# The latents' feed-forward by one level of Strassen's algorithm, in a two-layer diffusion backbone on one core

## The chip, the cores and the metric

The kernel runs on one core of one Trainium2 chip. A core has TensorE (matrix products, from SBUF into PSUM), VectorE, ScalarE and GpSimd (elementwise work; GpSimd reaches SBUF alone) and SyncE, whose queue issues all of this kernel's transfers. In the profile they are PE, DVE, ACT, POOL and SP; PEld is TensorE's loading of weights. The metric is the device time of one execution in microseconds (us). Before the change the median of three runs is 3615.9 us (3615.09 to 3621.17).

## The reference

Two layers work on 1024 latent tokens ("latents") of width 1024 and 256 context tokens. Each layer is an attention mixer and a convolutional feed-forward, each followed by a residual and a LayerNorm, with shift, scale and gate vectors that a small projection of the conditioning vector gives ("modulation"). The change is in the feed-forward, of inner width 2816:

```python
def conv_ffn(h, w_gate, w_up, conv_w, conv_b, w_down):
    g = h @ w_gate
    gp = jnp.pad(g, ((0, 0), (1, 1), (0, 0)))
    g = gp[:, :-2] * conv_w[0] + gp[:, 1:-1] * conv_w[1] + gp[:, 2:] * conv_w[2] + conv_b
    return (jax.nn.silu(g) * (h @ w_up)) @ w_down
```

Around it stand `h_l = xl * (1.0 + sc2_l) + sh2_l` and `xl = layer_norm(ALPHA * xl + gt2_l * f_l, ln2_g[i], ln2_b[i])`. Layer 0 does this for latents and context with the same weights, layer 1 for the latents alone, as only they are returned. All is float32.

## The kernel before

Activations lie with features on the 128 partitions and tokens along the free axis, in three tiles (`TT`): tile 0 and tile 1 are 512 latents each, tile 2 the 256 context tokens. A product in float32 is made of three faster ones: each operand is split into a rounded high part (`hi`, a ScalarE copy, L82) and the rest (`lo`, a subtraction on GpSimd or another engine, L85), and `gemm3` (L90) adds high times high, high times low and low times high in PSUM, every matmul at L88. So each weight block costs a split of 128x1024 (`weight`, L198), and each normalized tile is kept as two tiles (`b0h`, `b0l` for tile 0, `b1*`, `b2*` for the others).

A layer runs so:

- `mixer_pass` (L1046) makes the output projection of the mixer into the residual `acc`; in layer 0 for tiles 2 and 0, and then for tile 1.
- `mixer_norm` (L1078) queues the LayerNorm of each tile (`norm`, L316; `norm_parts`, L395) on a list `behind`. Each `gemm3` step calls `tick` (L100), which emits one step of the first norm in that list: the norms run behind matmuls. In layer 0 tile 2's norm is queued ahead of tile 0's.
- `conv_ffn` (L1097) loops over 22 blocks of 128 inner features. For each block it makes gate and convolution inputs per tile (`gate`, L1130), the convolution on VectorE (`conv`, L1141), up and the product with it, split again (`hidden`, L1148), and then the way down, whose 8 results per tile are added to `acc` by VectorE (`down`, L1157, L1170). Inner values never leave SBUF. The latents take 2*2*8*3 = 96 matmuls of 512 columns for gate and up in each block and 2*8*3 = 48 for the way down; the context takes 72 of 256 columns.
- In layer 0 the modulation vectors of layer 1 are summed on VectorE within that loop (`mod_vectors`, L161; L176), from 96 pieces of `w_mod`.
- At the end of layer 0 `finish` (L1188) queues the norms for the next mixer; `odd_begin` starts it with tiles 0, 2, 1. At the end of layer 1 the last tile is cut in two halves, so that the norm that nothing covers has 256 columns (`final`, L1173).

A planner orders each engine's instructions from this program by priority and by when it expects their inputs; `ahead` raises the priority of weights' loads. It also places the semaphore waits. The order on an engine is fixed when the kernel is built.

Of the kernel before, what the change touches and what calls it, by code (L numbers as in the profile page):

```python
# [12 lines left out]
F32 = mybir.dt.float32  # L13
# [5 lines left out]
P = 128  # L19
# [31 lines left out]
class Net:  # L51
# [109 lines left out]
    def mod_vectors(self, l, chunks, wpool, ppool, ptag):  # L161
# [3 lines left out]
        for which, half, cs in chunks:  # L165
            acc = {c: self.t(wpool, [P, 512], tag=f"mv{c}", bufs=1) for c in cs}
            c0 = 1024 * which + 512 * half
            for k in range(KT):
                w = self.t(wpool, [P, 512], tag="wm", bufs=2)
# [96 lines left out]
    def spread(self, tmp, ppool, ptag, r, nb, room=4, pbufs=None):  # L266

        nc = self.nc
        dg = self.t(tmp, [P, room, P], tag="diag", bufs=1)
# [125 lines left out]
    def norm_parts(self, t, eps, v, keep, done=None):  # L395
# [21 lines left out]
        if done is not None:  # L417
            done()

# [658 lines left out]
def mixer_norm(N, l, t):  # L1078

    scale = ALPHA if l == 0 else 1.0  # L1080
    N.behind.append((t, N.norm_parts(t, LN_EPS / scale**2, N.aff[t // 2], True)))
# [7 lines left out]
def mixer_out(N):  # L1089
    mixer_begin(N, 0)  # L1090
    for tiles in ((2, 0), (1,)):
        drain(mixer_pass(N, 0, tiles, N.qq, "f"))
        for t in tiles:
            mixer_norm(N, 0, t)


def conv_ffn(N, l):  # L1097
    nc, ins = N.nc, N.ins
    qq = N.qq
    sf = N.pool("scratch_f")  # L1100
    tiles = (0, 2, 1) if l == 0 else (0, 1)
    last = NF - 1
    tail = last if l == 0 else last - 1
    sm = N.pool("scratch_m")
    width = 1026 if l else 1284
    base = [1, 513, 1027]
    edges = [0, 1025] + ([] if l else [1026, 1283])
    cw = lambda i, f: N.vecs[:, V_CW + 66 * l + 22 * i + f : V_CW + 66 * l + 22 * i + f + 1]
    cb = lambda f: N.vecs[:, V_CB + 22 * l + f : V_CB + 22 * l + f + 1]
    hidh = N.t(sf, [P, TOK], F32R, tag="hidh", bufs=1)  # L1110
    hidl = N.t(sf, [P, TOK], F32R, tag="hidl", bufs=1)
    s = N.t(sf, [P, width], tag="s", bufs=1)
    for c in edges:
        nc.vector.memset(s[:, c : c + 1], 0.0)

    def padded():
        g = N.t(sf, [P, width], tag="g", bufs=2)
        for c in edges:
            nc.vector.memset(g[:, c : c + 1], 0.0)
        return g  # L1120

    def gemm(wt, t, c0=0, w=None):
        w = w or TT[t][1]
        ps = N.t(qq, [P, 512], tag="f")
        hh, hl = N.h[t]
        N.gemm3(ps[:, :w], [(wt[0][:, k * P : (k + 1) * P], wt[1][:, k * P : (k + 1) * P],
                             hh[:, k, c0 : c0 + w], hl[:, k, c0 : c0 + w]) for k in range(KT)])
        return ps[:, :w]

    def gate(wt, t, f, g, begin=True, s=s):  # L1130
        c = slice(base[t], base[t] + TT[t][1])
        ps = gemm(wt, t)
        nc.scalar.activation(g[:, c], ps, AF.Copy)
        if begin:
            nc.scalar.activation(s[:, c], ps, AF.Identity, scale=cw(1, f), bias=cb(f))

    def begin(t, f, g):
        c = slice(base[t], base[t] + TT[t][1])
        nc.scalar.activation(s[:, c], g[:, c], AF.Identity, scale=cw(1, f), bias=cb(f))

    def conv(f, g, s=s):  # L1141
        n = width - 2
        for sh, i in ((0, 0), (2, 2)):
            nc.vector.scalar_tensor_tensor(s[:, 1 : 1 + n], g[:, sh : sh + n], cw(i, f), s[:, 1 : 1 + n],
                                           op0=ALU.mult, op1=ALU.add)
        nc.scalar.activation(s[:, 1 : 1 + n], s[:, 1 : 1 + n], AF.Silu)

    def hidden(ps, t, c0=0, eng=None, out=None, s=s):  # L1148
        w = ps.shape[-1]
        t0 = TT[t][0] + c0  # L1150
        y = s[:, base[t] + c0 : base[t] + c0 + w]
# [21 lines left out]
    def final(wd, t, c0, w):  # L1173
# [3 lines left out]
        for m, _ in enumerate(down(wd, t, c0, w)):  # L1177
            if m % 2:
                next(steps)
# [675 lines left out]
```

## Time and profile before

| what | us |
| --- | --- |
| median of 3 runs | 3615.9 |
| the profiled execution | 3614.6 |
| its span, first to last instruction | 3612.8 |
| last matmul of layer 0's output projection | 903.4 |
| first feed-forward, last matmul | 1886.7 |
| last matmul of layer 1's output projection | 2809 |
| second feed-forward, last matmul of the way down | 3582.4 |
| mean clock granted to TensorE | 0.971 |

A row of a group gives line, engine, operation, what it writes <- what it reads, shapes and the count; behind the bar the busy time and the mean duration of one in ns; behind the next the idle time before them and who ended it. A row of the timeline begins with the start and the duration in us. In the view by stretches each engine has its busy time in the stretch and, in brackets, its instructions. Matmuls overlap each other, so the time that one costs is the distance from start to start.

### The profile page before, as it was taken

Reading aid. Unit: us, or ns where it says so; the run is one execution under the profiler, and the core shown is the slowest. Engines: PE = TensorE matmul, PEld = TensorE weight load, DVE = VectorE, ACT = ScalarE, POOL = GpSimd, SP = SyncE. Lnnn points to the kernel's source line nnn. Section 1 sums busy time; section 2 is a strip of 40 time slices with the busy share of each in tenths; the row PEclk is TensorE's granted clock in tenths of the full one; section 3 lists DMA queues with packets and bytes.
Section 4 is the critical chain, followed back from the end, with each engine's and each line's share of the span. In section 5 each row is a group of like instructions: output and inputs, shape, how many; then the busy total and the mean of one; then the engine's idle time right before and its main releaser. Section 6 shows DMA issues by size and latency. Waiting matters only on the chain.

```text
span 3612.8 us, 47500 instructions
## 1 busy us (share of the span) xinstructions
PE 3377.0 (93%) x17736; PEld 2779.2 (77%) x17736; DVE 2201.4 (61%) x3938; ACT 1428.1 (40%) x2667; POOL 1283.0 (36%) x956
## 2 busy tenths in 40 slices
PE   8998999999799999999987999998998999999996
PEld 4566778887688888888866888877886688888885
DVE  2137878865567556565455477777996544444445
ACT  3126778853422222222223355556774322222222
POOL 4244433324622222222247133445334522222224
PEclk9999999999999999999988999999999999999997
DMA  7666142332112222121113845557543111111111
GB/s 224 198 212 185 65 101 68 81 115 70 36 59 88 70 77 79 62 76 38 39 43 103 255 139 155 152 164 216 165 131 126 53 41 53 47 47 47 47 47 47
DMA packets 203864, 363.03 MB, mean 100 GB/s; under 512 B 16432, under 2 KB 102896, under 8 KB 202096
## 3 DMA queue, kind: packets, MB, share of 16 engines
q1 hardware_dynamic: 203632, 359.98, 32.6%
q8 instruction: 140, 2.29, 0.3%
q14 instruction: 92, 0.75, 0.1%
HBM read 284.61 MB, written 75.30 MB: 100 GB/s over the span
## 4 chain that ended last, share of the span: by engine, by line
PE 56%; POOL 7%; DVE 5%; issue 3%; ACT 3%; DMA 2%; SPq 0%; POOLq 0%; ACTq 0%; DVEq 0%
PE f L88 45%; PE tp L88 4%; PE s L88 2%; PE o L88 2%; POOL affy L405 1%; POOL acc L346 1%; PE tp L467 1%; POOL wl L85 1%; DVE stat L1573 1%; DVE p L1587 1%; DVE ptl L85 1%; POOL acc L413 1%; POOL sum L336 1%; ACT wh L82 1%; POOL acc L216 1%
## 5 line engine op out<-in xcount | busy, mean ns | idle before, releaser
L1170 DVE SCALAR_TENSOR_TENSOR acc<-f,modv,acc 128x512 f32<-128x512 f32 (+1 forms) x856 | 551.1, 691 | 398.2 <-PE f L88 396.2
L85 POOL TENSOR_TENSOR wl<-wraw,wh 128x1024 fp32r<-128x1024 f32 x122 | 299.4, 2454 | 925.7 <-ACT wh L82 925.6
L82 ACT ACTIVATE wh<-wraw 128x1024 fp32r<-128x1024 f32 x167 | 175.9, 1054 | 605.0 <-PE f L88 554.3
L88 PE MATMUL f<-b1h,wh 128*128 128x512 f32 (+1 forms) x848 | 338.4, 399 | 7.7 <-ACT wh L82 4.1
L88 PE MATMUL f<-b1l,wh 128*128 128x512 f32 (+1 forms) x848 | 337.0, 397 | 8.7 <-DVE b1l L85 8.6
L88 PE MATMUL f<-b1h,wl 128*128 128x512 f32 (+1 forms) x848 | 336.6, 397 | 2.7 <-DVE wl L85 2.7
L88 PE MATMUL f<-b0h,wh 128*128 128x512 f32 x784 | 313.4, 400 | 9.7 <-ACT wh L82 9.7
L88 PE MATMUL f<-hidl,wdh 128*128 128x512 f32 (+1 forms) x848 | 316.4, 373 | 3.0 <-POOL hidl L85 3.0
L88 PE MATMUL s<-k,q 128*128 128x512 f32 (+2 forms) x1152 | 305.7, 387 | 14.4 <-ACT sxc L1563 6.6
L88 PE MATMUL f<-hidh,wdh 128*128 128x512 f32 (+1 forms) x848 | 318.1, 375 | 0.2 <-ACT hidh L82 0.2
L88 PE MATMUL f<-b0h,wl 128*128 128x512 f32 x784 | 312.1, 398 | 5.0 <-POOL wl L85 5.0
L88 PE MATMUL f<-hidh,wdl 128*128 128x512 f32 (+1 forms) x848 | 315.1, 372 | 0.0
L88 PE MATMUL f<-b0l,wh 128*128 128x512 f32 x784 | 312.4, 398 | 0.0
L85 DVE TENSOR_TENSOR ptl<-tp,pth 128x512 fp32r<-128x512 f32 x412 | 279.6, 684 | 41.2 <-ACT pth L471 35.5
L471 ACT ACTIVATE pth<-tp 128x512 fp32r<-128x512 f32 x412 | 241.9, 594 | 104.0 <-PE tp L467 96.7
L467 PE MATMUL tp<-ident,p 128*128 128x128 f32 x1648 | 257.3, 276 | 20.3 <-DVE ptl L85 10.1
L467 PEld LDWEIGHTS tp<-ident,p 128*128 128x128 f32 x1648 | 197.4, 142 | 52.3 <-DVE ptl L85 10.3
L1153 DVE TENSOR_TENSOR s<-s,f 128x512 f32<-128x512 f32 (+1 forms) x112 | 69.8, 626 | 275.4 <-PE f L88 269.3
L88 PE MATMUL o<-pth,v 128*128 128x256 f32 x976 | 232.4, 300 | 4.6 <-ACT pth L471 4.4
L85 POOL TENSOR_TENSOR hidl<-s,hidh 128x512 fp32r<-128x512 f32 (+1 forms) x103 | 121.8, 1184 | 300.4 <-ACT hidh L82 287.7
L88 PEld LDWEIGHTS s<-k,q 128*128 128x128 f32 (+1 forms) x1152 | 188.7, 192 | 43.6 <-ACT p L1576 9.9
L88 PEld LDWEIGHTS f<-b1l,wh 128*128 128x128 f32 x848 | 162.3, 191 | 49.9 <-DVE b1l L85 14.4
(392 smaller groups left out, 8124.6 us busy)
## 6 DMA issues: line engine op xcount, KB each, us to landing
wm<-w_mod SPq DMA_DIRECT2D x192, 256.0 KB, 3.4
wraw<-w_gate SPq DMA_DIRECT2D x44, 512.0 KB, 3.5
wraw<-w_up SPq DMA_DIRECT2D x44, 512.0 KB, 3.5
wraw<-w_down SPq DMA_DIRECT2D x44, 512.0 KB, 3.5
k<-k SPq DMA_DIRECT2D x32, 640.0 KB, 5.3
v<-v SPq DMA_DIRECT2D x16, 1280.0 KB, 8.5
wraw<-w_in SPq DMA_DIRECT2D x39, 512.0 KB, 4.4
wraw<-w_out SPq DMA_DIRECT2D x32, 512.0 KB, 3.6
```

The lines of the kernel that those rows point to most:

```text
L82: return self.nc.scalar.activation(out, src, AF.Copy)
L85: (eng or self.nc.gpsimd).tensor_tensor(out, src, hi.bitcast(F32), op=ALU.subtract)
L88: self.nc.tensor.matmul(out, lhsT, rhs, start=start, stop=stop)
L216: nc.gpsimd.tensor_tensor(r[:rows, :w], r[:rows, :w], sin, op=ALU.mult)
L336: eng.tensor_tensor(new, acc[g], src, op=ALU.add)
L346: nc.gpsimd.tensor_tensor(x[k], x[k], c[:, :w], op=op)
L405: nc.gpsimd.tensor_scalar(y[:, :w], x, v[:, 0, k : k + 1], v[:, 1, k : k + 1], op0=ALU.mult, op1=ALU.add)
L413: nc.gpsimd.tensor_scalar(x, x, v[:, 2, k : k + 1], v[:, 3, k : k + 1], op0=ALU.mult, op1=ALU.add)
L467: nc.tensor.transpose(ps[:, n * P : (n + 1) * P], pt[:, kc : kc + P], N.ident[:, :])
L471: nc.scalar.activation(h[:, : n * P], ps[:, : n * P], AF.Copy)
L1153: nc.vector.tensor_tensor(y, y, ps, op=ALU.mult)
L1170: nc.vector.scalar_tensor_tensor(a, ps[:, :w], gt[:, m : m + 1], a, op0=ALU.mult, op1=ALU.add)
```

## The change

The feed-forward of the latents is written as two products of 2x2 blocks. On the way up the left matrix has gate and up weights as its rows and the two halves of the input features as its columns; the right matrix has the two halves of the features as rows and tiles 0 and 1 as columns. On the way down the halves are those of the inner width and of the output features. Each such product takes seven products of halves (Winograd's form, P1 to P7), of sums of blocks, in place of eight.

- `norm_operands` builds, in tile 1's norm, the sums and differences of the right matrix, split in high and low parts, for P3, P4, P5, P6 and P7. P1 and P2 need tile 0 alone and are done for the first 8 blocks ahead of that (`EARLY`), with their results stored in DRAM.
- `run_up` makes, block after block, the seven products, adds them out of PSUM, does the convolution and Silu on 1024 tokens, multiplies with up on GpSimd and stores the inner values in DRAM (`hid_d`). The weights' sums are made on VectorE from the raw blocks, and each of seven halves is split. The sums of `w_down` blocks for the way down are made here too, every second block, and stored in DRAM.
- `run_down` makes each of the seven products over 11 blocks of the inner width, into four PSUM banks, and splits a weight half and an inner half (or a sum of halves) for each step. The inner values come back from DRAM, into the places of the operands.
- The residuals of the norms before wait in DRAM meanwhile, and in layer 0 the context's operands as well.
- `context` does the context's feed-forward by plain products, last in layer 0, over the 22 blocks with all weights read and split again. The norms of tiles 0 and 1 run behind it.
- Tile 0's norm now comes ahead of tile 2's in layer 0, `odd_begin` takes tiles 0, 1, 2, the pools of weights are released and allocated anew around the feed-forward, and in layer 1 the last norm has 512 columns.

The core of the diff ("..." marks what is left out):

```diff
+        def pair(k):
...
+            nc.scalar.activation(ya, xa, AF.Identity, scale=v0[0], bias=v1[0])
+            pool.tensor_scalar(yb, xb, v0[1], v1[1], op0=ALU.mult, op1=ALU.add)
+            sub(vec, a, ya, f32(h0[0][:, k, :]))
+            sub(vec, a, a, f32(h0[1][:, k, :]))
+            self.hi(b22[0][:, k, :], yb)
+            self.hi(t1[0][:, k, :], a)
+            b, c = room(), ya
+            sub(vec, b, yb, a)
+            sub(pool, c, yb, ya)
+            self.lo(b22[1][:, k, :], yb, b22[0][:, k, :], vec)
+            self.lo(t1[1][:, k, :], a, t1[0][:, k, :], vec)
+            self.hi(t2[0][:, k, :], b)
+            self.hi(t3[0][:, k, :], c)
+            self.lo(t2[1][:, k, :], b, t2[0][:, k, :], vec)
+            sub(vec, b, f32(h0[0][:, k + 4, :]), b)
+            vec.tensor_tensor(b, b, f32(h0[1][:, k + 4, :]), op=ALU.add)
+            self.hi(t4[0][:, k, :], b)
+            self.lo(t3[1][:, k, :], c, t3[0][:, k, :], pool)
+            self.lo(t4[1][:, k, :], b, t4[0][:, k, :], pool)
...
+    ORDER = ("P1", "P2", "P6", "P7", "P5", "P4", "P3")
+    EARLY = 8
+    RING = 6
...
+        self.steps = first + early + rest + down
...
+    def split(self, src, eng=None):
+        N = self.N
+        h = N.t(self.pw, [P, 512], F32R, tag="ah", bufs=self.RING)
+        lo = N.t(self.pw, [P, 512], F32R, tag="al", bufs=self.RING)
+        N.hi(h[:, :], src)
+        N.lo(lo[:, :], src, h[:, :], eng)
+        return h, lo
...
+        if p == "P1":
+            src = a11
+        elif p == "P2":
+            src = a12
+        elif p == "P6":
+            s[1] = self.add(a21, a22, ALU.add)
+            src = s[2] = self.add(s[1], a11, ALU.subtract)
+        elif p == "P7":
+            src = self.add(a11, a21, ALU.subtract)
+        elif p == "P5":
+            src = s[1]
+        elif p == "P4":
+            src = a22
+        else:
+            src = self.add(a12, s[2], ALU.subtract)
+        self.parts[n] = self.split(src)
...
+        def finish(f):
+            x = g[f % 2]
+            nc.scalar.activation(s, x, AF.Identity, scale=cw(1, f), bias=cb(f))
+            nc.vector.scalar_tensor_tensor(s[:, 1:], x[:, : SEQ - 1], cw(0, f), s[:, 1:], op0=ALU.mult, op1=ALU.add)
+            nc.vector.scalar_tensor_tensor(s[:, : SEQ - 1], x[:, 1:], cw(2, f), s[:, : SEQ - 1], op0=ALU.mult, op1=ALU.add)
+            nc.scalar.activation(s, s, AF.Silu)
+            nc.gpsimd.tensor_tensor(v, v, s, op=ALU.mult)
+            N.load(self.hid_d[f][:, :], v)
...
+            self.advance(n)
+            ps = N.t(N.qq, [P, 512], tag="f")
+            (ah, al), (bh, bl) = self.parts.pop(n), N.op[p]
+            for k in range(4):
+                c = slice(k * P, (k + 1) * P)
+                N.mm(ps[:, :], ah[:, c], bh[:, k, :], k == 0, False)
+                N.mm(ps[:, :], ah[:, c], bl[:, k, :], False, False)
+                N.mm(ps[:, :], al[:, c], bh[:, k, :], False, k == 3)
+                N.tick()
+            evacuate(n, f, p, ps[:, :])
+            if n >= self.n_first:
+                next(mods, None)
+                if p == "P6" and f % 2:
+                    self.down_sums(f // 2)
...
+        def evacuate(p, d, ps):
+            y = q[:, d, :]
+            if p == "P1":
+                nc.scalar.activation(y, ps, AF.Copy)
+            elif p == "P2":
+                more(0, 0, d, ps)
+                more(0, 0, d, y)
+            elif p == "P6":
+                nc.vector.tensor_tensor(y, ps, y, op=ALU.add)
+                more(1, 0, d, y)
...
+            for d in range(4):
+                c = slice(d * P, (d + 1) * P)
+                ps = banks[d][:, :]
+                N.mm(ps, ah[:, c], bh[:, :], j == 0, False)
+                N.mm(ps, ah[:, c], bl[:, :], False, False)
+                N.mm(ps, al[:, c], bh[:, :], False, j == last)
+                N.tick()
+                if j == last:
+                    evacuate(p, d, ps)
+            if j == last and p in ("P4", "P3"):
+                ready(0 if p == "P4" else 1)
...
+        for f in range(NF):
+            g, s = room[:, 2 * (f % 2), :], room[:, 2 * (f % 2) + 1, :]
+            ps = gemm(parts_of(3 * f))
...
+            nc.scalar.activation(s, s, AF.Silu)
+            parts_of(3 * f + 1)
+            ps = gemm(parts[3 * f + 1])
+            drain(pending)
+            parts_of(3 * f + 2)
+            nc.vector.tensor_tensor(s, s, ps, op=ALU.mult)
...
 def conv_ffn(N, l):
...
+    ff.run_up(mods)
+    drain(mods)
...
+    ff.run_down(finish if l == 0 else answer)
     if l == 0:
...
+        ff.context()
         finish(2)
```

In the up stage a step is one product for one block (12 matmuls); `advance` prepares the splits up to six steps ahead (three on the way down, where a step takes two splits). On the way down VectorE makes the low parts of the inner values, and P6, P7, P5 and P4 take 2, 1, 1 and 3 sums of inner halves per step.

More of the change, by code (lines that the diff above doesn't have):

```diff
@@ L1080, in mixer_norm, with store @@
     scale = ALPHA if l == 0 else 1.0
-    N.behind.append((t, N.norm_parts(t, LN_EPS / scale**2, N.aff[t // 2], True)))
+    t0, w = TT[t]
+    def store():
+        N.load(N.res_d[l][t].rearrange("(k p) n -> p k n", p=P), N.acc[t][:, :, :])
+        if t == 2:
+            for x in range(2):
+                N.load(N.h2_d[x], N.h[2][x][:, :, :].bitcast(F32))
+    v = N.aff[t // 2]
+    make = N.norm_operands(v, store) if t == 1 else N.norm_parts(t, LN_EPS / scale**2, v, True, store)
+    if t == 1:
+        make = N.norm(1, 0, w, LN_EPS / scale**2, make)
+    N.behind.append((t, make))
 def drain(gen):
@@ L1092, in mixer_out @@
         drain(mixer_pass(N, 0, tiles, N.qq, "f"))
-        for t in tiles:
+        for t in sorted(tiles):
             mixer_norm(N, 0, t)
-def conv_ffn(N, l):
[L1098 to L1151, printed above, removed]
-        hh, hl = out or [x[:, t0 : t0 + w] for x in (hidh, hidl)]
-        nc.vector.tensor_tensor(y, y, ps, op=ALU.mult)
-        N.hi(hh, y)
-        N.lo(hl, y, hh, eng)
-    def down(wd, t, c0=0, w=None):
-        w = w or TT[t][1]
-        t0 = TT[t][0]
-        gt = N.mod(l, 5, t // 2)
-        if not isinstance(wd[0], tuple):
-            wd = ((wd, hidh[:, t0 : t0 + TT[t][1]], hidl[:, t0 : t0 + TT[t][1]]),)
-        for m in range(KT):
-            c = slice(m * P, (m + 1) * P)
-            ps = N.t(qq, [P, 512], tag="f")
-            N.gemm3(ps[:, :w], [(ws[0][:, c], ws[1][:, c], hh[:, c0 : c0 + w], hl[:, c0 : c0 + w])
-                                for ws, hh, hl in wd])
-            a = N.acc[t][:, m, c0 : c0 + w]
-            nc.vector.scalar_tensor_tensor(a, ps[:, :w], gt[:, m : m + 1], a, op0=ALU.mult, op1=ALU.add)
-            yield
-    def final(wd, t, c0, w):
-        steps = N.norm(t, c0, w, LN_EPS, stages(t, c0, w), "last")
-        next(steps)
-        for m, _ in enumerate(down(wd, t, c0, w)):
-            if m % 2:
-                next(steps)
-            yield
-        for _ in steps:
-            yield
-            with N.ahead(-100):
-                N.tick()
-    run = drain
@@ L1217, in conv_ffn @@
-    chunks = [(i, half, (0, 1) if i < 2 else (0,)) for i in range(6) for half in range(2)]
-    mods = N.mod_vectors(1, chunks, sm, qq, "f") if l == 0 else iter(())
-    early = tiles[:-1]
-    wg, g = weights("w_gate", 0), padded()
-    for t in early:
-        N.settle(t)
-        gate(wg, t, 0, g)
-    wu = N.weight(sf, ins["w_up"][l, 0], tag="wd", sbufs=1, raw=N.wp)
-    held = {t: gemm(wu, t) for t in early}
-    wg1, g1 = weights("w_gate", 1), padded()
-    for t in early:
-        gate(wg1, t, 1, g1, False)
@@ L1262, in conv_ffn, with answer @@
[L1262 to L1290 removed]
+    def answer(t):
+        N.behind.append((t, N.norm(t, 0, 512, LN_EPS, stages(t))))
@@ L1709, in mixer_end @@
     mixer_norm(N, 1, 1)
+    N.wp.release()
 def body(tc, ins, outs):
```

443 lines of the change are left out of this document (339 added, 104 removed).

## The prediction

> **What bounds the kernel now.** I read the page from the top, then the stretches that the change touches, then single instructions.
>
> ```profile
> span 3612.8 us, 47500 instructions
> PE 3377.0 (93%) x17736; PEld 2779.2 (77%) x17736; DVE 2201.4 (61%) x3938; ACT 1428.1 (40%) x2667; POOL 1283.0 (36%) x956
> PEclk9999999999999999999988999999999999999997
> GB/s 224 198 212 185 65 101 68 81 115 70 36 59 88 70 77 79 62 76 38 39 43 103 255 139 155 152 164 216 165 131 126 53 41 53 47 47 47 47 47 47
> ```
>
> TensorE is busy 93% of the span. The view by stretches shows where it is the bound: 1000 to 1840 (first feed-forward) and 2860 to 3553 (second) have it busy without a hole at clock 1.00, with VectorE at 59% and 47%. Around them (the two starts, the hand-over to layer 1, the end) it waits, at a lower clock.
>
> ```profile
> core 0: us, PE busy (x) PEld busy (x) DVE busy (x) ACT busy (x) POOL busy (x), PEclk, DMA share, GB/s
> 903.00:960.00 57.00, 39.22 (x193) 31.26 (x192) 28.49 (x37) 25.79 (x40) 43.60 (x34) 0.85 0.09 28
> 1000.00:1840.00 840.00, 840.00 (x4355) 712.91 (x4354) 492.35 (x789) 185.46 (x258) 207.45 (x117) 1.00 0.20 64
> 1886.00:1974.00 88.00, 55.48 (x227) 42.87 (x226) 54.75 (x89) 31.26 (x54) 63.23 (x58) 0.81 0.27 86
> 2860.00:3553.00 693.00, 693.00 (x3019) 561.58 (x3018) 324.30 (x464) 162.18 (x210) 200.42 (x104) 1.00 0.14 45
> 3553.00:3613.00 60.00, 27.13 (x143) 23.52 (x141) 35.02 (x74) 19.21 (x41) 33.33 (x42) 0.67 0.21 71
> ```
>
> A matmul's own duration (0.39) overlaps its neighbours, so I price it from start to start. TensorE's timeline, 512 columns, then 256:
>
> ```profile
> 1001.65 0.39 PE L88 MATMUL f<-b0h,wh 128*128 128x512 f32 x1
> ...
> 1007.22 0.40 PE L88 MATMUL f<-hidh,wdh 128*128 128x512 f32 x1
> 782.45 0.28 PE L88 MATMUL f<-b2h,wh 128*128 128x256 f32 x1
> ...
> 785.33 0.40 PE L88 MATMUL f<-b0h,wh 128*128 128x512 f32 x1
> ```
>
> 24 in 5.57 us and 24 in 2.88 us: 0.232 and 0.120 us each.
>
> **What is removed.** Per block of 128 inner features gate and up take 96 matmuls over the latents and will take 7 products of 12, 84; the way down takes 1056 in a layer and will take 924. That is 22*12+132 = 396 per layer, 792 in all, at 0.232: 184 us. The context's matmuls stay (22*72*0.120 = 190 us) but move to a stage of their own.
>
> The Trainium skill, "TensorE: Matmul & The Clock Gate", section "Back-to-back issue gap", gives 131 ns for a matmul of 512 columns in a sustained stream; by it the saving would be an estimated 104 us. The rows above have 232 ns, and they decide.
>
> **What is added** is elementwise work. Its prices, from the groups by shape, the instructions of the modulation sums (first duration row: min/median/max) and what VectorE waited for there:
>
> ```profile
> L85 POOL TENSOR_TENSOR wl<-wraw,wh 128x1024 fp32r<-128x1024 f32 x38 | 91.3, 2403 | 273.9 <-ACT wh L82 273.9
> L346 POOL TENSOR_TENSOR acc<-acc,bcs 128x512 f32<-128x512 f32 x12 | 15.3, 1302 | 15.5 <-ACT bcs L341 15.5
> L1144 DVE SCALAR_TENSOR_TENSOR s<-g,vecs,s 128x1024 f32<-128x1024 f32 x38 | 49.0, 1290 | 0.7
> L1153 DVE TENSOR_TENSOR s<-s,f 128x512 f32<-128x512 f32 x39 | 26.8, 688 | 92.9 <-PE f L88 92.9
> L1170 DVE SCALAR_TENSOR_TENSOR acc<-f,modv,acc 128x256 f32<-128x256 f32 x152 | 62.9, 476 | 77.4 <-PE f L88 77.4
> L176 DVE SCALAR_TENSOR_TENSOR mv<-wm,siluc,mv x112: 736/747/2889, 798.7 to 1617.1; 128x512 f32<-128x512 f32 x112
>   DMA wm<-w_mod: 57.4, 35
> ```
>
> And one more resource. GpSimd's and VectorE's timelines during a norm:
>
> ```profile
> 951.95 3.34 POOL L405 TENSOR_SCALAR affy<-acc,aff 128x512 f32<-128x512 f32 x3
> 955.26 1.31 POOL L413 TENSOR_SCALAR acc<-acc,aff 128x512 f32<-128x512 f32 x1
> 956.55 1.52 POOL L405 TENSOR_SCALAR affy<-acc,aff 128x512 f32<-128x512 f32 x2
> 952.74 0.69 DVE L85 TENSOR_TENSOR b1l<-affy,b1h 128x512 fp32r<-128x512 f32 x1 [1.42 <-POOL affy L405]
> 953.36 0.68 DVE L348 TENSOR_TENSOR acc<-acc,f 128x512 f32<-128x512 f32 x1
> 955.32 0.69 DVE L85 TENSOR_TENSOR b1l<-affy,b1h 128x512 fp32r<-128x512 f32 x1 [0.59 <-POOL affy L405]
> 957.36 1.27 DVE L85 TENSOR_TENSOR b1l<-affy,b1h 128x512 fp32r<-128x512 f32 x1 [1.35 <-POOL affy L405]
> ```
>
> GpSimd's op takes 0.76 alone (1.52 for two), but 1.31 at 955.26, where a VectorE op with two inputs in SBUF runs beside it; VectorE's takes 0.69, but 1.27 at 957.36, behind GpSimd's. The op at 953.36, with one input in PSUM, takes 0.68 beside GpSimd. So the two take turns when VectorE reads two SBUF tiles: such an op of 512 holds GpSimd up 1.31-0.76 = 0.55 us, some 0.14 less than its duration. I count a turn as 0.55 (512, two tiles), 1.15 (1024, the convolution), 0.60 (a modulation sum), and GpSimd's full 1.30 (512) or 2.40 (1024). Before, 1000 to 1840 has 207 us of GpSimd and few such ops, all under cover of TensorE. After:
>
> A whole block in the up stage: TensorE 84*0.232 = 19.5 us. GpSimd seven low parts and one product of 1024: 11.5. VectorE four sums for the weights, two sums for the way down (four every second block), two convolution ops, seven additions out of PSUM: 6*0.69+2*1.29+7*0.69 = 11.6; its turns 6*0.55+2*1.15 = 5.6. Turns in all 17.1: hidden under 19.5. ScalarE's seven high parts are shorter still.
> One of the first eight blocks, whose P1 and P2 are done ahead: TensorE 60*0.232 = 13.9, VectorE one addition less, 10.9; turns 5*1.30+2.40+5.6 = 14.5, so 14.5.
> A product on the way down: TensorE 132*0.232 = 30.6; turns 11*(1.30+0.55) = 20.4, with P6's 22 sums and four accumulations from SBUF 34.9, with P4's 33 sums 38.5. That is 12 over; three steps (8 us) are prepared ahead; I take 3 per layer.
>
> The traffic through DRAM (inner values, sums, partial products, residuals, weights read twice) is some 72 MB more per layer by the tile sizes and the context's weights again: over 700 us some 100 to 150 GB/s beside 47 now, where the page shows a slice of 255. I cost it at nothing: the last block's P6 to P3 (14 us) cover the first fetches of inner values for the way down; without that cover 4 MB cost some 16 us at 255 GB/s. On SyncE's queue each block's store waits for GpSimd's product and the weights' loads stand behind it, but those lead by a block (19.5 us). The working tiles of the up stage lie where tile 1's residual was and wait for its store, and VectorE's additions for P5 with them; a store of that size:
>
> ```profile
> x<-acc SPq DMA_DIRECT2D x2, 2048.0 KB, 7.7
> ```
>
> P6 and P7 and the eight banks (8*2.8 us) cover 7.7.
>
> **Starts and ends**, on TensorE's and VectorE's timelines:
>
> ```profile
> 903.36 0.40 PE L88 MATMUL f<-b1h,wl 128*128 128x512 f32 x1
> 913.42 0.80 PE L88 MATMUL f<-b0h,wh 128*128 128x512 f32 x1 [9.66 <-ACT wh L82]
> 942.77 2.48 DVE L348 TENSOR_TENSOR acc<-acc,f 128x512 f32<-128x512 f32 x4 [1.85 <-ACT bcs L341]
> 1971.39 0.51 PE L88 MATMUL f<-b1l,wh 128*128 128x512 f32 x1 [1.66 <-DVE b1l L85]
> 2809.10 0.40 PE L88 MATMUL f<-b0h,wh 128*128 128x512 f32 x1
> 2830.11 2.48 DVE L348 TENSOR_TENSOR acc<-acc,f 128x512 f32<-128x512 f32 x4 [2.80 <-ACT bcs L341]
> 3582.42 0.28 PE L88 MATMUL f<-lateh,wd2l 128*128 128x256 f32 x1
> ```
>
> Tile 1's norm reaches its last multiplications 39 us after the output projection ends in layer 0 (903.4 to 942.8), 21 us in layer 1 (2809.1 to 2830.1). There the five operand sets are built: per pair of slices eight VectorE ops with two SBUF inputs and GpSimd's three of 1.30 and two of 0.76: 8*0.55+5.4 = 9.8 in turns, 39 for four pairs, and with some six weight splits among them 47. P1 and P2 of eight blocks (192*0.232 = 44.5 us) cover the norm, not this. So P6 starts 86 us after 903.4 and 68 after 2809.1: TensorE idles some 40 and 23 us.
>
> **Layer 1**, from 2809.1: 68, a restart at half clock 5, up 8*14.5+14*19.5 = 389, down 7*30.6+3 = 217, tile 0's norm against P3 4, the last norm uncovered. Now the end shows 30.4 us after the last matmul (3582.4 to 3612.8) for 256 columns; for 512 I take 21 to the multiplications and 14 for the rest: 35. Sum 718, ending at 3527: 86 earlier.
>
> **Layer 0**, from 903.4: 86. Then 48 steps carry the modulation of layer 1: TensorE 48*12*0.232 = 134; VectorE 8*10.9+11.6 and 128 sums of 0.747 (the sixteen first ones are no longer than that), 195; turns 8*14.5+17.1+128*0.60 = 210, so the bound there; with the waits for w_mod (57.4 us) on VectorE as well, 267. I take 220, near the turns, as six steps prepared ahead absorb part of the waits. Thirteen blocks more: 254. Six products: 184+3 = 187. P3 and the context: TensorE 31+190 = 221; per context block turns are 4*1.30+2*0.55 and three short ones, 7.2 of 8.64 us, VectorE 8*0.476+3.1 = 6.9; but two norms fall here, each with 33 us of turns (GpSimd 10*1.30, 12*0.76 and 1.0, VectorE 18*0.55): between 221 and 287, I take 262, as they come together early. Then layer 1's first projections to where 1971.4 stands: four units of latents 0 and two of latents 1 (24 matmuls of 0.232 each), two of the context and a value projection (144 of 0.120) are 51 us of matmuls, now spread over 85; tiles 0 and 1 will be ready and the context's norm covered, but the weights' buffers come free late: 62. Sum 86+220+254+187+262+62 = 1071, at 1974: 3 later.
>
> In all 86-3 = 83 less: span 3530. The execution profiled took 3614.6, 1.8 more than its span, and the median of the runs, 3615.9, is 1.3 above it: forecast 3533.
>
> **Rivals.**
> TensorE alone sets the pace (the turns find cover, modulation slides into free time): layer 0 86+384+184+221+55 = 930 (-138), layer 1 68+384+214+33 = 699 (-105), 243 less: 3373. For it: the scheduler started modulation sums at 798.7, far ahead of their place. Against: 210 us of turns do not fit in 134.
> Each VectorE op holds GpSimd for its whole duration (0.69, 1.29, 0.75): the modulation steps +28, P6 and P4 +11 a layer, the operand sets +4 a layer, layer 1's first blocks (15.6 each) +9, the context +7, 74 in all: 3607. The 0.14 at 955.26 speaks against it, from one op. The Trainium skill, "SBUF — State Buffer", section "Who interferes with whom", says that the second to issue is fully blocked; the rows show most, not all of it.
> Slower: VectorE's queue becomes the bound in both up stages, on the way down and in the context, because each of its two-input ops finds GpSimd in the middle of an op (0.65, half of 1.30). Modulation steps 195+200*0.65 = 325 against 220: +105; P6 and P4 33 and 44 ops at 1.34, 103 against 64: +39 a layer; the context 6.9+5*0.65 = 10.1 against 8.64 a block: +33; layer 1's first blocks +13: 3533+229 = 3762. It passes no change from 0.24 us per op. For it: at 957.36 such a wait was 0.58. Against: GpSimd is idle 40% of a whole block, and an op that waits leaves GpSimd at work.
> In the context alone: its splits stand behind Silu and the inner values on ScalarE, 2.5 us late for up and for the next gate, 22*5 = 110 on 221, under which the norms' turns find room: 331 against 262, 3602. Against: ScalarE now takes a later weight ahead of an earlier block's work:
>
> ```profile
> 1110.48 1.06 ACT L82 ACTIVATE wh<-wraw 128x1024 fp32r<-128x1024 f32 x1 [7.35 <-PE f L88]
> 1111.45 0.58 ACT L1133 ACTIVATE g<-f 128x512 f32<-128x512 f32 x1
> ```
>
> That fewer matmuls do not come out: the count would not be some 792 under 17736 (a few records can lack).
>
> **How the numbers follow.** Forecast 0.44 (its own range 3470 to 3580, from the bounds of the modulation steps and the context), TensorE alone 0.13, whole durations 0.15, VectorE's queue 0.18, the context 0.06, an exact balance 0.04. Whole durations and the context end near the bound of 0.2% (7 us, about what a measurement here can tell): half of the one and a third of the other I count as no change. Faster 0.44+0.13+0.08+0.04 = 0.69, same 0.04+0.07+0.02 = 0.13, slower 0.18. The range 3430 to 3640 takes in both of these and the weaker half of the other two; their far ends, 3373 and 3762, lie outside.
>
> **What would show it.** TensorE idle before the first P6 some 40 and 23 us; a step in layer 0's modulation near 4.6 us against 2.8 later; whole blocks at 19.5 us and clock 1.00; products at 30.6; the context some 10.5 us a block; 35 us after the last matmul. Steps longer than 2.8 in whole blocks, or VectorE over 90% busy there, would prove me wrong; so would TensorE waiting for DMA.

## The result, and the profile after

The changed kernel takes 3731.6 us (median of four runs, 3725.5 to 3736.1) against 3618.5 us beside it: ratio 1.0311, 95% interval 1.029 to 1.0331. It is 3.1% slower; forecast was 3533 us, 2.3% faster. The profiled execution has a span of 3727.8 us, 115.0 more than before.

The page of the changed kernel, its first lines and the granted clock in 40 slices:

```profile
span 3727.8 us, 49048 instructions
PE 3273.4 (88%) x16844; PEld 2667.7 (72%) x16844; DVE 2668.0 (72%) x4124; ACT 1653.1 (44%) x3153; POOL 1802.2 (48%) x1316
PEclk9999999998777899999799999999999889999997
```

The matmuls did become fewer (17736 records before), and TensorE is busy 104 us less. VectorE is busy 467 us longer and GpSimd 519. TensorE, at 93% before, is at 88% of a longer span: it waits, and the clock sags where it waits most (slices 11 to 14, mainly the first feed-forward's modulation). The view by stretches, in order: the 48 modulation steps, the whole blocks, then P1, P2, P6, P7, P5 and P4 of the way down, P3, the context; and layer 1's first products, up stage, way down and end:

```profile
core 0: us, PE busy (x) PEld busy (x) DVE busy (x) ACT busy (x) POOL busy (x), PEclk, DMA share, GB/s
985.00:1272.00 287.00, 180.77 (x702) 145.84 (x702) 224.02 (x304) 57.30 (x78) 104.88 (x64) 0.77 0.58 185
1275.00:1523.00 248.00, 248.00 (x1069) 201.30 (x1068) 186.00 (x188) 84.42 (x124) 157.89 (x99) 1.00 0.41 135
1523.00:1577.00 54.00, 37.31 (x135) 27.07 (x134) 25.24 (x24) 16.74 (x28) 19.28 (x12) 0.87 0.94 360
1577.00:1607.00 30.00, 30.00 (x133) 24.82 (x133) 15.39 (x14) 13.17 (x23) 14.67 (x11) 1.00 0.29 90
1607.00:1642.00 35.00, 32.17 (x135) 24.48 (x135) 34.79 (x39) 13.14 (x23) 19.29 (x12) 1.00 0.29 83
1642.00:1672.00 30.00, 30.00 (x134) 24.86 (x133) 28.28 (x32) 12.78 (x23) 15.62 (x11) 1.00 0.34 97
1672.00:1704.00 32.00, 29.66 (x130) 23.93 (x129) 31.57 (x35) 12.38 (x22) 16.36 (x11) 1.00 0.40 124
1704.00:1744.00 40.00, 33.79 (x136) 25.90 (x136) 39.29 (x49) 12.75 (x23) 16.87 (x11) 0.96 0.37 123
1744.00:1801.00 57.00, 44.99 (x151) 33.02 (x150) 37.45 (x42) 26.49 (x44) 45.29 (x34) 0.79 0.22 62
1801.00:2034.00 233.00, 205.93 (x1607) 199.36 (x1607) 204.09 (x336) 123.86 (x240) 153.04 (x109) 0.93 0.50 164
...
2929.00:3015.00 86.00, 60.88 (x226) 46.29 (x226) 60.14 (x63) 38.49 (x67) 69.95 (x50) 0.82 0.45 144
3015.00:3419.00 404.00, 387.90 (x1644) 308.95 (x1643) 301.82 (x312) 129.79 (x193) 255.49 (x156) 1.00 0.44 145
3419.00:3689.00 270.00, 235.64 (x946) 182.46 (x944) 205.79 (x225) 99.89 (x171) 132.23 (x92) 0.94 0.42 144
3689.00:3728.00 39.00, 7.94 (x21) 4.57 (x20) 17.12 (x23) 8.72 (x14) 17.25 (x15) 0.55 0.15 54
```

The whole blocks of layer 0, and its P2 and P7, run as TensorE's own pace has it (19.5 us a block, 30 us a product). Most of the rest is longer than its matmuls. Set against the terms of the prediction, by the starts of the matmuls at each border:

| term | predicted us | measured us |
| --- | --- | --- |
| layer 0: to the first P6 | 86 | 81 |
| 48 steps with modulation | 220 | 287 |
| 13 whole blocks | 254 | 251 |
| six products of the way down | 187 | 221 |
| P3 and context | 262 | 290 |
| to where 1971.4 stood | 62 | 52 |
| between the layers | 838 | 843 |
| layer 1: to a running P6 | 73 | 86 |
| up | 389 | 404 |
| way down with tile 0's norm | 221 | 270 |
| end | 35 | 39 |

The differences add up to 197, with 1 us that layer 0's attention ended later: the 198 us between the span of 3530 forecast and 3727.8. Three terms carry most: modulation (+67), the ways down (+34 and +49) and P3 with the context (+28).

What TensorE waited for in the modulation steps, from the view of waits (us in total, times, longest), and the group of these matmuls:

```profile
PE f L183 <- DVE sum L176: 100.4, 10, 18.4
```

```profile
L183 PE MATMUL f<-ones,sum 128*128 128x1 f32 x128 | 25.7, 322 | 100.4 <-DVE sum L176 100.4
```

And the group of VectorE's sums, over the same stretch, and before the change over 1000 to 1840:

```profile
L176 DVE SCALAR_TENSOR_TENSOR sum<-affy,siluc,sum 128x512 f32<-128x512 f32 x112 | 99.6, 916 | 11.1 <-DMA affy<-w_mod 10.4
```

```profile
L176 DVE SCALAR_TENSOR_TENSOR mv<-wm,siluc,mv 128x512 f32<-128x512 f32 x98 | 92.2, 960 | 51.8 <-DMA wm<-w_mod 51.4
```

L183 is TensorE's own part of the modulation, which totals a sum over the partitions. It stands in TensorE's queue directly behind the step in which its last sum is called. Ten times in 287 us TensorE stands still before it, for 100 us together; the 128 matmuls of the totals are busy for 26 us themselves. A sum has not become dearer: its mean is 0.92 us, against 0.96 in the stretch before the change. The 0.75 that the prediction took is the median, which is the same in both kernels; some sums took far longer, up to 2.89 us in both.

What GpSimd's low parts and VectorE's operations cost each other in layer 1's up stage, where there is no modulation, by groups:

```profile
L85 POOL TENSOR_TENSOR al<-sum,ah 128x512 fp32r<-128x512 f32 x84 | 124.9, 1506 | 95.8 <-ACT ah L82 91.0 <-DVE u L1364 4.9
L1391 DVE SCALAR_TENSOR_TENSOR acc<-acc,vecs 128x1023 f32<-128x1023 f32 x21 | 26.9, 1283 | 20.7 <-ACT acc L1390 20.7
L1392 DVE SCALAR_TENSOR_TENSOR acc<-acc,vecs 128x1023 f32<-128x1023 f32 x21 | 43.1, 2052 | 0.5
L1254 DVE TENSOR_TENSOR sum<-raw,sum 128x512 f32<-128x512 f32 x21 | 31.4, 1497 | 14.9 <-POOL al L85 14.9
```

And what TensorE waited for in its slow blocks there (3085 to 3215):

```profile
PE f L88 <- POOL al L85: 14.0, 11, 2.6
```

The two convolution operations are alike. The first takes 1.28 us, its price alone; the second finds GpSimd at work and takes 2.05. The sum for P3's weights takes 1.50 against 0.69. GpSimd's low part takes 1.51, only 0.21 over its price of 1.30; the turns of a whole block had charged GpSimd 5.6 us for its eight operations, 0.70 each. So much of the hold-up falls on VectorE. Here the low parts of GpSimd come late enough that TensorE waits for them.

On the way down TensorE waits for VectorE's low parts instead, and hardly for GpSimd's. One of a sum of inner halves takes 1.02 us, and 0.70 in the run below that leaves GpSimd's low parts out. From 1523 to 1750 the waits for GpSimd's are 0.6 us; the group of VectorE's, and what TensorE waited for it:

```profile
L85 DVE TENSOR_TENSOR al<-sum,ah 128x512 fp32r<-128x512 f32 x44 | 44.9, 1023 | 3.0 <-ACT ah L82 2.7
```

```profile
PE f L88 <- DVE al L85: 15.8, 17, 2.2
```

### The profile page after: what moved, and what is told of

It reads as the page before. It is cut to its first block, busy times and chain, and to the rows that moved or that the text cites. A ratio compares the mean times of both kernels' runs of the same rounds, so it can differ in the third digit from the quotient of the medians.

```text
span 3727.8 us, 49048 instructions
## 1 busy us (share of the span) xinstructions
PE 3273.4 (88%) x16844; PEld 2667.7 (72%) x16844; DVE 2668.0 (72%) x4124; ACT 1653.1 (44%) x3153; POOL 1802.2 (48%) x1316
## 5 line engine op out<-in xcount | busy, mean ns | idle before, releaser
L85 POOL TENSOR_TENSOR al<-raw,ah 128x512 fp32r<-128x512 f32 x374 | 561.8, 1510 | 352.7 <-ACT ah L82 335.9
L82 ACT ACTIVATE ah<-raw 128x512 fp32r<-128x512 f32 x418 | 255.1, 624 | 349.2 <-PE f L88 143.6
L85 POOL TENSOR_TENSOR al<-sum,ah 128x512 fp32r<-128x512 f32 x176 | 261.3, 1500 | 270.7 <-ACT ah L82 265.8
L88 PE MATMUL s<-k,q 128*128 128x512 f32 (+2 forms) x1152 | 306.7, 388 | 14.5 <-ACT sxc L1858 6.6
L88 PE MATMUL f<-al,ah 128*128 128x512 f32 x616 | 255.2, 414 | 33.2 <-DVE al L85 33.1
L88 PE MATMUL f<-ah,ah 128*128 128x512 f32 x616 | 247.9, 410 | 25.1 <-ACT ah L82 24.8
L88 PE MATMUL f<-ah,al 128*128 128x512 f32 x616 | 250.4, 407 | 3.2 <-POOL al L85 3.2
L88 PE MATMUL o<-ptl,v 128*128 128x256 f32 x656 | 186.0, 295 | 17.6 <-DVE ptl L85 16.7
L85 POOL TENSOR_TENSOR wl<-wraw,wh 128x1024 fp32r<-128x1024 f32 x36 | 91.1, 2530 | 205.6 <-ACT wh L82 203.7
L88 PEld LDWEIGHTS o<-pth,v 128*128 128x128 f32 x976 | 171.6, 192 | 24.1 <-ACT pth L544 7.9
L88 PE MATMUL f<-T,ah 128*128 128x512 f32 x528 | 170.1, 404 | 0.2 <-DVE u L1364 0.2
```

Of the source, the lines that this page charges most:

```text
L82: return self.nc.scalar.activation(out, src, AF.Copy)
L85: (eng or self.nc.gpsimd).tensor_tensor(out, src, hi.bitcast(F32), op=ALU.subtract)
L88: self.nc.tensor.matmul(out, lhsT, rhs, start=start, stop=stop)
```

## The experiments

My theory after the result ("own queue") was that TensorE's time is lost where something stands in a queue directly behind work that is late: its totals of the modulation, and the loads of P1's weights behind bulk loads. The rival ("turns") was that VectorE and GpSimd hold each other up by more than I had counted. Each run was timed beside the kernel before on the same chip. The changed kernel's ratio is 1.0311; "gain" below is against its 3731.6 us.

**Modulation on every third step.**

```diff
-                next(mods, None)
+                if (n - self.n_first) % 3 == 0:
+                    next(mods, None)
```

> The modulation sums of layer 1 are called at every third step of the up stage instead of at each of the first 48. Theory 'own queue': TensorE's matmuls of the modulation (ones|sum) stand in its queue directly behind sums that VectorE makes late; they cost 100 us of TensorE waits between 985 and 1275. Spread over 138 steps, VectorE has 12+4.7 us of work in a block of 19.5, so the waits shrink to some 2 to 3 us per group of sums (12 groups): layer 0's up stage falls from 538 us to 410 to 430, the kernel to 3605 to 3625. Rival 'VectorE's queue' (each op with two SBUF inputs waits 0.65 us for GpSimd, wherever it stands): about 24 us a block, up stage 500, the kernel 3690 to 3700.

3750.2 us, ratio 1.0361 (1.0338 to 1.0385): slower than the changed kernel. Layer 0's up stage took 576 us in place of 538. Both theories had expected a gain. TensorE's waits for sums between 989 and 1565:

```profile
PE f L183 <- DVE sum L176: 132.9, 10, 48.0
```

Still ten waits, but the last alone takes 48 us and stands at the border of the stage. 48 calls at every third step need more than its 138 steps; the last ones are made at its end, and their pieces of `w_mod` were issued behind the first loads of the way down, on SyncE's timeline:

```profile
1545.62 14.88 SPq L75 DMA_DIRECT2D affy<-w_mod  x4
```

Up to that border the run was ahead: the stage's last matmul started 526 us after the first P6, in the changed kernel 538. So spreading gained some 11 us, far less than either theory had asked, and the border took more than that back. The other nine waits add up to 85 us, against 100 for all ten in the changed kernel: the totals wait although VectorE has less to do in a block. That they wait because each stands right behind its last sum is what the next run tests.

**Totals two or three steps later.** The sums stay where they were, in alternating buffers.

```diff
+                if k == 5 and late:
+                    self.mod_total(*late)
                 if k % 2 and k < KT - 1:
                     yield
-            ps = self.t(ppool, [P, 512], tag=ptag)
...
+            late = l, which, half, cs, acc, ppool, ptag
             yield
+        self.mod_total(*late)
```

> The sums stay at the first 48 steps, with the same VectorE work, but the matmuls that total a group come two to three steps after its last sum. Theory 'own queue': the 48 steps fall from 290 us to what VectorE is busy there, 227 to 245, the kernel to 3675 to 3690. Rival 'VectorE's work is the bound anyway' (busy or held up by GpSimd throughout): no more than 10 us gained, 3720 or above.

3717.7 us, 1.0269 (1.0247 to 1.0291): 14 us gained. The 48 steps took 259 us, between the two expectations, but the 90 steps behind them took 265 in place of 251, so half of the 28 us was lost again. The waits for sums fell to 74.5 us:

```profile
PE f L195 <- DVE sum L180: 45.0, 5, 18.0
...
PE f L195 <- DVE opt L180: 29.5, 4, 15.9
```

The place of the totals is a part of the cost, not all of it.

**Inner values by halves.** Left halves of all inner values first, then the right halves and the residuals, all before P1.

```diff
-            N.load(y, self.hid_d[h * half + i][:, :])
+            N.load(y[:, :512], self.hid_d[h * half + i][:, :512])
...
+            for i in range(NF):
+                N.load(self.hid[i][:, 512:], self.hid_d[i][:, 512:])
+            self.load_residual(0)
             self.load_residual(1)
```

> The way down first loads the left halves of all inner values (all that P1 and P2 read), then the right halves, and the two residuals last. Theory 'bulk ahead': P1's steps wait for weights and inner values that share the DMA engines with 9.5 MB which nobody needs yet; P1 falls from 53 us to 31 to 36 in both layers, the kernel to 3690 to 3700. Rival 'SyncE's queue': the loads are late because they stand behind stores and weights that wait for buffers; then P1 stays above 45 us and the kernel gains under 15 us.

3744.2 us, 1.0335 (1.0309 to 1.0362): nothing gained; P1 took 56 us in both layers. By itself this read as the rival's case. But its SyncE timeline shows the right halves still issued ahead of P1's last weight (the one at 3452.81) and the residuals ahead of P2's, so the edit had not moved what it was meant to move:

```profile
3449.38 2.35 SPq L75 DMA_DIRECT2D b1h<-hid  x4
3452.09 0.32 SPq L75 DMA_DIRECT2D b1l<-hid  x1
3452.81 0.33 SPq L75 DMA_DIRECT2D raw<-w_down  x1
3453.43 1.01 SPq L75 DMA_DIRECT2D b1l<-hid  x2
3454.80 1.26 SPq L75 DMA_DIRECT2D acc<-res  x2
3456.20 20.62 SPq L75 DMA_DIRECT2D raw<-w_down  x7
```

**Bulk loads late.** The same halves, the rest spread over the steps that follow.

```diff
+            if p == "P1" and j == 8:
+                self.load_residual(0)
+            if p == "P2" and j < 6:
+                for i in (2 * j, 2 * j + 1):
+                    if i < NF // 2:
+                        for f in (i, i + NF // 2):
+                            N.load(self.hid[f][:, 512:], self.hid_d[f][:, 512:])
+            if p == "P2" and j == 8:
+                self.load_residual(1)
```

> As in the run with the halves, but the right halves of the inner values are now issued step by step in P2, tile 0's residual at the ninth step of P1 and tile 1's at the ninth of P2; in the run with the halves SyncE still issued them ahead of P1's weights. Theory 'bulk ahead': P1 falls from 53 us to 33 to 40 in both layers, the kernel to 3695 to 3710. Rival 'SyncE's order and the ring of four raw weights': P1 stays above 45, the kernel above 3718.

3699.3 us, 1.0225 (1.0209 to 1.024): 32 us gained. P1 took 30.0 and 34.2 us in place of 53.8 and 52.5; P6, whose right halves came later now, 39 in place of 34.7. "Bulk ahead" holds. The DMA view of the changed kernel, 3405 to 3475 (traffic in 40 slices; KB each, median us from issue to landing):

```profile
GB/s 23 293 262 30 135 254 61 104 324 353 346 398 419 407 392 406 405 405 396 389 405 411 393 407 404 399 414 418 414 412 410 400 400 382 391 389 375 133 7 150
...
raw<-w_down SPq DMA_DIRECT2D x15, 256.0 KB, 8.9
```

For 45 us the queues move some 400 GB/s, and a weight half lands 8.9 us after its issue. Over the same part it lands after 5.1 us in the run with late bulk, but after 5.3 in the run with the halves too, whose P1 was no shorter:

```profile
raw<-w_down SPq DMA_DIRECT2D x20, 256.0 KB, 5.1
```

```profile
raw<-w_down SPq DMA_DIRECT2D x15, 256.0 KB, 5.3
```

So the time to landing is not what P1 gained by. What differs is when a weight is issued: P1's last one 19 us after its first matmul with late bulk, 36 us after it in the run with the halves.

**No low parts on GpSimd.** The low parts of the weights are left out: ScalarE makes two copies in place of a high and a low part.

```diff
-        N.lo(lo[:, :], src, h[:, :], eng)
+        if eng is None:
+            N.hi(lo[:, :], src)
+        else:
+            N.lo(lo[:, :], src, h[:, :], eng)
```

> The low parts of the weights in the feed-forward are left out: ScalarE writes a second copy of the weight where GpSimd subtracted, so GpSimd has only the norms, the products of 1024 and a few sums, and VectorE nearly never meets it. Theory 'own queue' and 'bulk ahead': only what GpSimd's turns cost in the stages goes: 128 modulation sums at 0.75 instead of 0.92 us (22 us), layer 1's five slow blocks (22), P6's and P4's extra (12 per layer): the kernel at 3650 to 3690. Rival 'turns of VectorE and GpSimd are behind most of the loss': 130 us or more gained, 3600 or below.

3593.1 us, 0.9922 (0.9895 to 0.9948): 138 us gained, as the rival asked. By stages: the 48 steps 263 us (23 less), layer 1's up stage with the start of P6 391 (34 less), P4 30.0 (9.5 less), P6 29.9 (4.8 less), P3 13 and 5 less, the context 10 less, and 11 less in layer 0 from the first P1 to the first P6. The two ways down together are 61 us shorter. So "turns" is the largest single cause, and "own queue" had priced it at 40 to 80. The run takes away GpSimd's own time as well as the hold-ups; the waits shown above say which of the two TensorE felt: GpSimd's lateness in layer 1's up stage, VectorE's on the way down. TensorE still waits for the modulation, and the mean of a sum fell by 0.10 us:

```profile
PE f L183 <- DVE sum L176: 82.4, 9, 17.0
```

```profile
L176 DVE SCALAR_TENSOR_TENSOR sum<-affy,siluc,sum 128x512 f32<-128x512 f32 x112 | 88.6, 818 | 14.6 <-DMA affy<-w_mod 13.7
```

18 of the 100 us of waits went with GpSimd's low parts; the rest has its cause elsewhere.

**Low parts on VectorE in the up stage.** A real version of the same.

```diff
-        self.parts[n] = self.split(src)
+        self.parts[n] = self.split(src, self.N.nc.vector)
```

> In the up stage the weights' low parts are made by VectorE instead of GpSimd, which keeps only the product of 1024. Theory 'turns': VectorE has 11.6+7*0.69 = 16.4 us in a block of 19.5 and nearly no turns: layer 1's slow blocks vanish (up stage from 3012 to 3419 becomes 380 to 392), the modulation stretch stays within 15 us of 287 (28 us more work, 25 us less waiting): the kernel 3695 to 3715. Rival 'VectorE's queue is the bound': the modulation stretch grows by 30 us or more and the kernel to 3745 or more.

3683.6 us, 1.0181 (1.0166 to 1.0196): 48 us gained, more than expected. Layer 1's up stage took 402 us from the first P6 in place of 425; the modulation steps 280, in spite of 53 low parts added to VectorE there. The rows that had grown, in this run's layer 1:

```profile
L1392 DVE SCALAR_TENSOR_TENSOR acc<-acc,vecs 128x1023 f32<-128x1023 f32 x21 | 26.8, 1277 | 0.0
L1254 DVE TENSOR_TENSOR sum<-raw,sum 128x512 f32<-128x512 f32 x21 | 14.4, 687 | 0.4
```

1.28 in place of 2.05, 0.69 in place of 1.50: both are back at the price that they have alone. With seven more operations per block VectorE holds TensorE up less than it did beside GpSimd.

**Modulation by TensorE.**

```diff
+                    nc.tensor.matmul(ps[at, :], self.siluc[:, k, :], w[:, :], start=k == 0, stop=k == KT - 1,
+                                     tile_position=(0, 32 * j))
```

> The modulation of layer 1 is made by TensorE (96 matmuls of siluc with the pieces of w_mod, two behind each of the same 48 steps) instead of VectorE sums and totals by TensorE; VectorE loses 128 operations with two SBUF inputs there. Theory 'VectorE stands before TensorE': the waits of TensorE for sums (100 us) and VectorE's 110 us go, TensorE gets 96*0.45 = 43 us more; the 48 steps fall from 287 us to 180 to 200, the kernel to 3625 to 3645. Rival 'weights and GpSimd limit that stretch' (loads of 24 MB of w_mod, GpSimd behind with the low parts): 48 steps stay above 230 us, the kernel above 3670.

3700.6 us, 1.0232 (1.0215 to 1.0249): 31 us gained; the 48 steps 259 us. By these figures the rival was right (above 230, above 3670), but not for its reason: the waits for sums are gone, and TensorE is busy 244 of 260 us, by the view by stretches:

```profile
983.00:1243.00 260.00, 243.90 (x776) 120.91 (x776) 128.63 (x152) 64.12 (x89) 95.41 (x64) 0.96 0.62 204
```

The matmuls of that line (duration min/median/max, first and last start):

```profile
L204 PE MATMUL f<-opt,siluc x96: 589/592/1061, 1000.8 to 1237.8; 128*32 128x512 f32 x96
L204 PE MATMUL f<-sum,siluc x96: 592/592/617, 1007.7 to 1242.6; 128*32 128x512 f32 x96
```

The 96 products in plain float32 are 192 matmuls, each 0.45 us from start to start: 87 us where I had put 43. The waits went, as the first theory said, but what replaced them was dearer. That is not all: with 44 us more its 180 to 200 would be 224 to 244.

**P1 and P2 ahead for 12 blocks.** `EARLY = 12` in place of 8.

> P1 and P2 are done ahead for 12 blocks instead of 8. Theory 'operand building is the wall before P6': TensorE fills 22 us of its wait of some 35 us (layer 0) and 25 to 30 us (layer 1) before P6, less what the eight more splits take from VectorE and GpSimd, and twelve blocks run at GpSimd's 14.5 instead of 13.9: the kernel 10 to 25 us faster, 3707 to 3722. Rival 'the splits delay the operands by as much': no change, 3725 to 3740.

3750.1 us, 1.036 (1.0344 to 1.0376): 18 us slower. P6 started 98 and 95 us after the first P1 in place of 75 and 64, 23 and 30 us later for 22 us of matmuls. Both expectations missed it: P6 came later by all that the additional products took. That their splits held up the building of the operands is the likely reason; it was not shown.

**One sum per step on the way down.**

```diff
+    DOWN = ("P1", "P2", "P5", "P6", "P7", "P4", "P3")
...
+        if p == "P5":
+            nc.vector.tensor_tensor(b12, b12, b11, op=ALU.subtract)
+            return b12
+        if p == "P6":
+            nc.vector.tensor_tensor(b12, b22, b12, op=ALU.subtract)
+            return b12
+        return self.add(*((b12, b11) if p == "P7" else (b21, b12)), ALU.subtract)
```

> On the way down P5 comes before P6 and the sums of inner halves are written over a half that is no longer needed, so that P5, P6, P7 and P4 take one sum per step each instead of 1, 2, 1 and 3. Theory 'turns': P6 and P4 fall from 34.7 and 39.4 us to 30 to 33 each, 11 to 14 us per layer, the kernel to 3703 to 3712. Rival 'the lead of three steps and the loads set P6 and P4': under 6 us per layer, 3720 or above.

3702.9 us, 1.0227 (1.0209 to 1.0245): 29 us gained, as expected. The four products took 124 us in place of 137 in layer 0 (P5 32.4, P6 29.9, P7 29.9, P4 32.0), and the same in layer 1.

**Together, with TensorE's modulation (z1), with VectorE's late totals (z2), and with those on every second step.** All three have late bulk (right halves over all of P2, tile 1's residual in P5), one sum per step and VectorE's low parts, on the way down too but for P3.

> All that helped together: the modulation by TensorE, bulk loads late, one sum per step, low parts of the weights by VectorE in the up stage and, but for P3, on the way down. If the causes are separate, their gains add up (31 + 32 + 25 + 48 us, and some 10 us that P6 lost when the bulk came late): 3575 to 3600, below the kernel before. Rival 'they are the same waits seen from several sides': above 3625.

> As z1, but with the modulation sums on VectorE as in the changed kernel, their totals two to three steps later. Theory 'turns': without GpSimd's low parts a sum takes 0.75 us instead of 0.92, but VectorE has 40 low parts more in that stretch, 195+28 us of work, so the 48 steps take 235 to 255 us against some 245 for z1: within 15 us of z1. Rival 'TensorE's waits for sums come back': 20 us or more slower than z1.

> As z2, with the modulation sums called at every second step, so over 96 steps in place of 48, and their totals still two to three calls later. Theory 'concentration': what the modulation still costs in z2 (48 steps 236 us against 150 in layer 1, which has none) is VectorE's work piled on 48 steps; spread, layer 0's up stage falls from 496 us to 450 to 475 and the kernel to 3530 to 3555. Rival 'the order on the queues, not the load': TensorE's totals meet late sums wherever they stand, as in the run with every third step; the up stage stays at 490 or above, the kernel at 3570 or above.

| run | us | ratio to before (interval) | layer 0: 48 steps, up stage | layer 1: up stage | P1 |
| --- | --- | --- | --- | --- | --- |
| changed kernel | 3731.6 | 1.0311 (1.029 to 1.0331) | 287, 538 | 425 | 53.8, 52.5 |
| z1 | 3580.9 | 0.9889 (0.9873 to 0.9905) | 245, 496 | 401 | 32.4, 31.7 |
| z2 | 3573.5 | 0.987 (0.9854 to 0.9887) | 236, 496 | 401 | 31.4, 32.4 |
| every second step | 3557.2 | 0.9831 (0.9813 to 0.9848) | -, 478 | 401 | 31.5, 31.9 |

z1's gains add up as separate causes should: 151 us, where its parts had given 31, 32, 29 and 48 by themselves, 140 in all. z2 stays within 15 us of z1, but its 158 us are more than its parts, 14, 32, 29 and 48, 123 in all. Whether late totals are worth more beside a quieter GpSimd, or the low parts of the way down, which had no run of their own, bring the rest, was not run. The last run beats both kernels: 1.7% faster than before. Its gain over z2 (17 us in the up stage) is short of what "concentration" asked for (20 us at least) and beyond what its rival allowed, so it decides for neither. Its page:

```profile
span 3556.1 us, 48344 instructions
PE 3242.5 (91%) x16844; PEld 2660.7 (75%) x16844; DVE 2677.4 (75%) x4498; ACT 1659.4 (47%) x3153; POOL 1168.6 (33%) x876
```

Its up stage of layer 0 in the view by stretches, and then what is left of TensorE's waits for the modulation:

```profile
978.00:1457.00 479.00, 430.21 (x1785) 345.74 (x1786) 435.72 (x636) 140.39 (x204) 60.87 (x23) 0.92 0.57 185
```

```profile
PE f L195 <- DVE opt L180: 16.3, 2, 12.8
...
PE f L195 <- DVE sum L180: 9.8, 2, 5.8
```

VectorE is busy as long as in the changed kernel (2677 against 2668 us) with 374 operations more, GpSimd 634 us less, and 172 us of the span are gone. Spreading the sums gained 11 us in the first experiment, before the border, and 17 here, where the calls end inside the stage. Whether the later totals, GpSimd's silence or the later loads make the difference was not run apart.

## Why the prediction was wrong

- **Fewer matmuls, 184 us: right.** 892 records less: the 792, 96 because layer 1's last way down no longer has 192 matmuls of 256 columns, and a few of the norms. Whole blocks at 19.5 us and clock 1.00 (layer 0) show the saving where nothing else stands in the way. That TensorE is busy only 104 us less goes with its mean clock, 0.94 against 0.971.
- **First P6: right in layer 0** (81 against 86), 13 short in layer 1, where TensorE took P6's first operands one by one as they came. In layer 0 it did so too: the first P6 took 11 us, which the table has in the modulation. That twelve blocks ahead were worse fits the step: P1 and P2 do not cover the building of the operands.
- **Turns as a sum of work: the step that failed.** I added up GpSimd's time and VectorE's turns, found 17.1 under 19.5 ("hidden under 19.5") and 14.5 beside 13.9, and counted no wait. The 13 whole blocks of layer 0 bore it out; the blocks with modulation, layer 1's whole blocks (19.5 to 25 us each) and the way down did not. In the sum I let VectorE's operations hold GpSimd up and never the other way round, though the row at 957.36 (1.27 in place of 0.69) showed it and stands in the prediction. In the changed kernel's trace of layer 1's up stage the weights' sums and the convolution on VectorE took 80 us longer than alone, GpSimd's operations 37 (an estimate: each duration less 0.69, 1.28, 1.29 or 2.40). The order on an engine is fixed, so an operation that waits 0.8 us delays all behind it, additions that free a bank and weight parts that TensorE is about to read among them. Taking GpSimd's low parts away gave 138 us: 61 on the two ways down, 34 in layer 1's up stage, which I had put at TensorE's pace but for 5 us, and 23 in the modulation.
- **Modulation, 220 taken from 210 to 267: mis-sized, 287.** A sum was priced by its median, 0.747, where its mean before was 0.96, and TensorE's totals were put at nothing. They stand in the queue of the engine that was to be kept busy: 100 us of waits, and 26 us busy, beside the 134 us of products. The remaining 27 us hold the slow first P6 and a clock of 0.77. Of the 67 us missing, the run without GpSimd's low parts gave 23 back in this stretch, and the later totals 28, of which 13 were lost again behind it (whether the two add up was not run).
- **DMA "at nothing": failed.** P6 to P3 of the last block did not cover the loads: P1 lost 23 and 22 us. I named 16 us as the price without cover, for 4 MB; but 22.6 MB move in those 70 us, as all that the way down needs was called at once. Late bulk brought P1 to 30 and 34.
- **P6 and P4: the sizes right** (34.7 and 39.4 against 34.9 and 38.5), the cover not. "Three steps (8 us) are prepared ahead; I take 3 per layer" should have been 12 to 15: the lead of three steps hid nothing that can be seen.
- **P3 and the context: 28 short.** The context took 10.5 us a block as forecast, all 22 of them, but tile 0's norm, which was to run beneath, lay on P3 (57 and 47 us for 31 of matmuls). Without GpSimd's low parts P3 took 13 and 5 us less; how the rest comes about no run took apart.
- **Rivals.** "VectorE's queue", 3762, came nearest, and for a part of its reason: one of the two convolution operations and one of the weights' sums did wait some 0.8 us each for GpSimd. But the mean modulation sum lost 0.10 us when GpSimd's low parts went, not 0.65, and the whole blocks of layer 0 covered what waits there were. "Whole durations" added to the same term, but 74 us in all, and again on GpSimd's side alone. The Trainium skill, "SBUF — State Buffer", section "Who interferes with whom", calls the ports that VectorE and GpSimd share an exclusive lock and says: "Issue order, not op shape, decides who blocks." The rows of L1392 (2.05 where it finds GpSimd at work, 1.28 without its low parts) and of GpSimd's low part (1.51 for 1.30) agree.

Open stays what the modulation still costs in the best run, and P3's wait for the norm.

## What to carry to other kernels

Trading matmuls for elementwise work needs more than a sum of work per engine: ask of each added operation what stands behind it in its queue, and whether two engines that work on the same memory will hold each other up in both directions. Take the mean, not the median, as the price of an operation in such a sum. A small total on the engine that sets the pace is better placed several steps after the work that it needs. And when a stage starts, load what its first product reads and let the rest follow step by step.

## What the runs showed of the hardware that was not expected

- Operations of VectorE with two operands in SBUF were held up by GpSimd by some 0.8 us in two groups (2.05 against 1.28, 1.50 against 0.69), GpSimd's low parts by 0.2 (1.51 against 1.30); giving the low parts of the up stage to VectorE was 48 us faster than sharing the work.
- Loads and stores from one queue hold some 400 GB/s for 45 us. A 256 KB load landed 8.9 us after its issue in the changed kernel, 5.1 and 5.3 in two runs that moved nearly as much (306 and 319 GB/s over those 70 us, against 323) in smaller pieces. The Trainium skill, "DMA: Bandwidth & Descriptors", section "Bandwidth", gives 425 GB/s for a load of 16 MB with one core at work; the slices here reach 419.
- A plain float32 matmul of 512 columns comes as two instructions of 0.45 us from start to start, together some four times the 0.232 us of one with rounded operands.
